# Mixer output projection of a streaming-encoder block: 2x2 blocks by seven products, branch results kept on chip

## Chip, cores and metric

One core of a Trainium2 chip. The metric is the device time of one execution in microseconds (us), from start to end, median of three runs.

## What is computed

One layer in float32 on 512 positions and 1024 channels. `mm` is matrix multiplication over channels; all weights lie in DRAM.

```python
h = rmsnorm(x, norm_mix_g);  z = h @ w_in                  # 1024 -> 7184
a = gmlp_spatial_gating(...); b = forgetting_attention(...)
y_a = a @ w_branch_a;  y_b = b @ w_branch_b                # 1024 -> 1024 each
merged = gate_a * y_a + gate_b * y_b                       # gates: sigmoids of columns of z
x = x + merged @ w_out                                     # the mixer's output projection
h2 = rmsnorm(x, norm_ffn_g);  up = h2 @ w_up               # 1024 -> 5632, then a causal convolution
x = x + (gelu(up[:, :2816]) * up[:, 2816:]) @ w_down
ple = p @ w_ple                                            # 256 -> 1024
x = x + ple * sigmoid(rmsnorm(x, norm_ple_g) @ w_ple_gate)
out = rmsnorm(x, norm_final_g)
```

## The kernel before

Every product is made at close to float32 precision from three passes: an operand is split into a rounded part "hi" and a remainder "lo", and lo*hi, hi*lo and hi*hi are added in a PSUM bank (`mm3`, L166 to L169, and L181/L183/L185, L243/L245/L247 for the two layouts). A matrix 512x1024 times 1024x1024 so takes 192 matmuls with 512 columns each. Splitting a weight piece is a cast on ACT for hi (L153), and for lo either a DVE subtraction (L159) or, with `sub="dma"`, an ACT negation of hi (L156) to which a DMA issued by POOL adds the raw weight (L157, "accumulating DMA"). hi and lo tiles come from a ring of five and one extra, the raw weights from a ring of three.

The order of TensorE's work (PE) is written by hand for most stages, that of ACT, DVE, POOL and of SP's DMA queue is set by a scheduler when the kernel is built; each engine then runs its own list strictly in order, and waits on semaphores for what the others make. Activations live in large SBUF slots numbered 0 to 7; a slot is used anew when its last reader is done.

The stages around the change, with the profile's lines:

- **Branch B** (PE until 432.3 us): eight column tiles of 24 matmuls; `store_b` multiplies the bank by a sigmoid gate (L1039) and POOL writes the result to DRAM as `gyb_d` (L1040). The gates come back from DRAM as `sg` tiles, four buffers (L1019).
- **Branch A** (432.3 to 475.8): the same with `w_branch_a`, whose operand aT is loaded from DRAM in four 1 MB pieces (L992). `store_a` multiplies by the gate (L1052), loads the branch B result (L1054), adds it (L1055) and splits the sum into hi and lo (L380/L381) as mT.
- **Output projection**: `proj_N` for the left 512 columns, 96 matmuls (L167 to L169), all four row blocks at a time; then `proj_N_steps` for the right 512 columns, 96 matmuls row block by row block (L243/L245/L247). `evac_x1` (L1071) adds each bank to x1, the residual. `w_out` comes through the raw ring in eight pieces, each lo made by DVE. In between stand transposes of p (L451) and, row block by row block, `rest[rb]()`: the normed row block is made (L468) and transposed on PE (L421) into h2T.
- **The w_ple product** (24 matmuls) and the **first up-projection**: two gate column tiles ("early"), in halves of 256 columns so that the first half can start before the last row block is there; then the two linear column tiles with 512 columns.
- After that up-projections, convolution and down-projections alternate to the end. The down-projection (L1216) already uses seven products in the place of eight for four groups of its inputs, with the sums for it made by DVE (`pair_parts`).

Of the kernel before, what the change touches and what calls it, by code (L numbers as in the profile page):

```python
# [43 lines left out]
def hybrid_block(  # L44
# [18 lines left out]
    def rows_bc(ap, n):  # L63
# [408 lines left out]
    def k_view(t, n=NK):  # L472
        return t[:, 0:n * 512].rearrange("p (k r) -> p k r", k=n)
# [496 lines left out]


    late_es, late = open_pool("late", "right")
    state["pool"][5] = state["pool"][6] = state["pool"][7] = state["late"] = late
    for i in (5, 6, 7):
        slot(i)
    aT = tuple(k_view(slot(i)) for i in (7, 6))
    cvT = late.tile([P, 2 * P], F32, tag="cvT", name="cvT")
    extra_es, state["extra"] = open_pool("extra", "right")
    for t in ("xhi", "xlo"):
        state["extra"].tile([P, 4, 256], F32R, tag=t, name=uid(t), bufs=1)  # L980
    scr_es, scr = open_pool("scrC", "right")

    oT = tuple(k_view(slot(i)) for i in (2, 3))
# [39 lines left out]
    def branch(wv, act, n0, use, sgs, py=None):  # L1023

        for n in range(0, NK, 2):
            nxt = gates_of(n0 + n + 2) if n0 + n + 2 < N_GATES else None
            py = py or pieces_T(wv, P * n)
# [8 lines left out]
    gyb_d = tc.dram_tile([D, S], F32, name="gyb_d")  # L1036

    def store_b(by, sg, c):
        V.tensor_tensor(sg, by, sg, ALU.mult)  # L1039
        G.dma_start(gyb_d[c * P:c * P + P, :], sg)  # L1040

    sgs = branch(w_b_v, oT, 0, store_b, gates_of(0), w_merge[1])

# [2 lines left out]
        T.transpose(bk[:, i * P:(i + 1) * P], cvr[i], ident)  # L1046
    V.tensor_copy(cvT, bk[:, :2 * P])

    mT = tuple(k_view(slot(i)) for i in (5, 2))
# [12 lines left out]

    scr_es, scr = open_pool("scrD", "right")
    x1 = slot(3, F32).rearrange("p (b c) -> p b c", b=NB)
    nc.sync.dma_start(x1, x2d.rearrange("(b q) c -> q b c", q=P))
    gffn = scr.tile([P, D], F32, tag="gbc", name="gffn", bufs=1)
# [14 lines left out]
    h2T = tuple(k_view(slot(i)) for i in (0, 1))  # L1081


    ple1 = slot(4, F32)[:, 0:2048].rearrange("p (b c) -> p b c", b=NB)
    prep = slot(7)
    pT = tuple(prep[:, 1024 * i:1024 * i + 1024].rearrange("p (k r) -> p k r", k=2) for i in range(2))
    prow = slot(6, F32)[:, 0:1024].rearrange("p (b c) -> p b c", b=NB)
    nc.sync.dma_start(prow, p2d.rearrange("(b q) c -> q b c", q=P))

    def evac_x1b(bk, rb, ch):  # L1090
        evac_x1(bk, rb, ch)
        ss1 = square_sum(bk, x1[:, rb, 512:], "s1")
        rest[rb] = rms_rows(x1[:, rb, :], half[rb], ss1, gffn, scr, h2T, rb)
# [5 lines left out]
    with tc.manual_schedule(engines={mybir.EngineType.PE}):  # L1099
        po = proj_N_steps(w_out_v, 0, NK, mT, 1, evac_x1b)  # L1100
        steps(po, 48)
        transpose_p(prow, pT, 0)
        steps(po, 12)
        rest[0]()
        steps(po, 24)
        rest[1]()
        pp = proj_N_steps(w_ple_v, 0, 2, pT, 1, evac_ple, subs=load_N(w_ple_v, 0, 2, 1))
        steps(po, 12)
        transpose_p(prow, pT, 2)
        w_up0 = [pieces_T(w_up_v, 0, V, "dma")]  # L1110

        up0 = [bank("mm") for _ in range(2)]
        early = chain(*(proj_T_steps(w_up0[0][i], h2T, up0[i], slice(0, 256)) for i in range(2)))
        steps(pp, 16)
        rest[2]()
        steps(pp, 8)
        steps(early, 18)
        rest[3]()
        w_up0.append(pieces_T(w_up_v, DFF, "dma"))
        run(early)  # L1120
        for i in range(2):
            run(proj_T_steps(w_up0[0][i], h2T, up0[i], slice(256, S)))
# [15 lines left out]


    N_SEVEN = 4  # L1140
    A11, A12, A22, S1, S2, S3, S4 = range(7)
    f_last, n_last = 4 * N_SEVEN, NF - 4 * N_SEVEN

    def pair_parts(e, o, t):
# [20 lines left out]
    def up_jobs(q, done):  # L1165

        ug = [None, None]

        def load(o):
            return lambda: pieces_T(w_up_v, o + 2 * q * P, "dma")  # L1170

        def gate(py):
            for i in range(2):
                if q == 0:
                    bk = up0[i]
                else:
                    bk = bank("mm")
                    proj_T(py[i], h2T, bk)
                ug[i] = conv(bk, 2 * q + i, "ug")
                A.activation(ug[i], ug[i], AF.Gelu_apprx_tanh)  # L1180

        def linear(py):
            uls = []
            for i in range(2):
                bk = bank("sc")
                proj_T(py[i], h2T, bk)
# [252 lines left out]
```

## Time and profile before

| | |
|---|---|
| median of 3 runs | 939.83 us (939.01 to 939.87) |
| profiled execution | 939.11 us, of which the span from first to last instruction is 937.3 |
| granted TensorE clock | 0.997 of full speed, mean of the span |
| busy: PE / DVE / ACT / POOL | 923.2 (98%) / 615.9 (66%) / 541.6 (58%) / 98.1 (10%) |
| DMA traffic | 155.84 MB, mean 166 GB/s |

Times in all views are microseconds from the start of the span. A matmul's printed duration is its time from issue to end, and matmuls overlap: the pace is the distance between two starts. "Idle before" in brackets at a row's end is how long the engine stood idle ahead of it, and who released it.

### The profile page before, as it was taken

To read this page: it belongs to the slowest core of one execution; us is meant where nothing else is said; L and a number is where in the kernel's file an instruction comes from. 1 tells how busy PE (TensorE), PEld (TensorE's weight loads), DVE (VectorE), ACT (ScalarE), POOL (GpSimd) and SP (SyncE) were. 2 spreads that over 40 slices of the span, in tenths; PEclk is the share of its full clock that TensorE was granted. 3 is DMA by queue.
4 is the path that set the end of the run, shared out by engine and by line. 5 is a ranking of instruction groups with operands and counts; after the bars stand their busy time and mean duration, and the time that the engine had idled before them with its cause. 6 is when DMAs were issued, how large, how long until landed. Compare 5 with 4: busy or idle time off the path is not lost.

```text
span 937.3 us, 12029 instructions
## 1 busy us (share of the span) xinstructions
PE 923.2 (98%) x4351; PEld 767.3 (82%) x4351; DVE 615.9 (66%) x1121; ACT 541.6 (58%) x868; POOL 98.1 (10%) x152
## 2 busy tenths in 40 slices
PE   8999999999999999999999999999999999999996
PEld 7878888888888888888888888888888888888885
DVE  6886899578777767535635438667666767454654
ACT  7755675477777777434424757656555655545633
POOL 1000001400000001000000211111111111100124
PEclk9999999999999999999999999999999999999998
DMA  9533273756444466399641896684856864975522
GB/s 338 190 91 124 68 205 101 239 154 164 125 116 115 111 158 164 112 352 365 212 156 46 194 258 151 175 192 114 219 139 153 213 149 113 230 233 143 112 69 90
DMA packets 109543, 155.84 MB, mean 166 GB/s; under 512 B 6308, under 2 KB 72028, under 8 KB 109484
## 3 DMA queue, kind: packets, MB, share of 16 engines
q1 hardware_dynamic: 97596, 112.83, 37.6%
q0 software_dynamic: 11744, 41.72, 21.6%
q8 instruction: 34, 0.56, 0.3%
q10 hardware_dynamic: 144, 0.52, 0.1%
q14 instruction: 25, 0.20, 0.1%
HBM read 107.84 MB, written 14.71 MB: 131 GB/s over the span
## 4 chain that ended last, share of the span: by engine, by line
PE 94%; DMA 3%; issue 1%; DVE 1%; ACT 0%; SPq 0%; DVEq 0%; POOLq 0%; POOL 0%
PE bank L181 18%; PE bank L183 18%; PE bank L185 18%; PE bank L1216 8%; PE bank L245 3%; PE bank L243 3%; PE bank L247 3%; PE bank L313 3%; PE bank L320 3%; PE bank L317 3%; PE bank L168 3%; PE bank L169 3%; PE bank L167 3%; PE bank L905 2%; PE bank L896 2%; PE bank L868 1%
## 5 line engine op out<-in xcount | busy, mean ns | idle before, releaser
L181 PE MATMUL bank<-slot,wlo 128*128 128x512 f32 (+1 forms) x664 | 263.4, 398 | 0.0
L183 PE MATMUL bank<-slot,whi 128*128 128x512 f32 (+1 forms) x664 | 258.1, 389 | 0.0
L185 PE MATMUL bank<-slot,whi 128*128 128x512 f32 (+1 forms) x664 | 257.8, 389 | 0.0
L153 ACT CAST whi<-raw 128x1024 fp32r<-128x1024 f32 x100 | 104.6, 1048 | 76.6 <-DMA raw<-in_w_up_dram 19.2
L185 PEld LDWEIGHTS bank<-slot,whi 128*128 128x128 f32 x664 | 124.7, 188 | 25.1
L181 PEld LDWEIGHTS bank<-slot,wlo 128*128 128x128 f32 x664 | 124.7, 188 | 20.6
L183 PEld LDWEIGHTS bank<-slot,whi 128*128 128x128 f32 x664 | 125.1, 188 | 19.6
L157 POOL DMA_DIRECT2D wlo<-raw x54 | 46.8, 866 | 538.8 <-ACT wlo L156 383.9
L159 DVE TENSOR_TENSOR wlo<-raw,whi 128x1024 fp32r<-128x1024 f32 x45 | 55.0, 1223 | 47.3 <-ACT whi L153 47.0
L1216 PE MATMUL bank<-whi,slot 128*128 128x512 f32 x192 | 61.7, 389 | 0.0
L156 ACT ACTIVATE wlo<-whi 128x1024 fp32r<-128x1024 f32 x54 | 57.0, 1059 | 1.0
L245 PE MATMUL bank<-wlo,slot 128*128 128x512 f32 x138 | 54.2, 393 | 0.5 <-DMA wlo<-raw 0.5
L243 PE MATMUL bank<-whi,slot 128*128 128x512 f32 x138 | 54.5, 395 | 0.0
L247 PE MATMUL bank<-whi,slot 128*128 128x512 f32 x138 | 54.1, 392 | 0.0
L1132 DVE SCALAR_TENSOR_TENSOR ul<-bank,cvT,ul 128x511 f32<-128x511 f32 x22 | 16.5, 750 | 41.4 <-ACT ul L1131 41.4
L1216 PEld LDWEIGHTS bank<-whi,slot 128*128 128x128 f32 x192 | 36.0, 188 | 7.4
L878 ACT ACTIVATE t<-t,mn 128x512 f32<-128x512 f32 (+1 forms) x64 | 35.8, 560 | 9.7 <-DVE mn L875 8.3
L265 DVE TENSOR_TENSOR wlo<-slot,whi 128x1024 fp32r<-128x1024 f32 x24 | 29.3, 1221 | 14.9 <-ACT whi L264 14.9
L1131 ACT ACTIVATE ul<-bank,cvT 128x512 f32<-128x512 f32 x22 | 17.1, 775 | 35.6 <-PE bank L185 35.6
L1216 PE MATMUL bank<-wlo,slot 128*128 128x512 f32 x96 | 37.3, 389 | 0.0
L1223 DVE TENSOR_TENSOR slot<-bank,slot 128x512 f32<-128x512 f32 x48 | 32.5, 683 | 5.0 <-PE bank L1216 4.7
L381 DVE TENSOR_TENSOR slot<-bank,slot 128x512 fp32r<-128x512 f32 x34 | 22.5, 684 | 17.8 <-ACT slot L380 17.7
(334 smaller groups left out, 1838.6 us busy)
## 6 DMA issues: line engine op xcount, KB each, us to landing
wlo<-raw POOLq DMA_DIRECT2D x54, 512.0 KB, 5.1
raw<-in_w_up_dram SPq DMA_DIRECT2D x44, 512.0 KB, 4.4
raw<-in_w_in_dram SPq DMA_DIRECT2D x36, 512.0 KB, 3.9
more<-in_w_in_dram SPq DMA_DIRECT2D x20, 512.0 KB, 8.2
slot<-in_w_down_dram SPq DMA_DIRECT2D x16, 512.0 KB, 3.7
raw<-in_w_branch_b_dram SPq DMA_DIRECT2D x8, 512.0 KB, 3.7
slot<-aT_d SPq DMA_DIRECT2D x4, 1024.0 KB, 9.8
sg<-gate_d SPq DMA_DIRECT2D x16, 256.0 KB, 5.2
```

Of the source, the lines that this page charges most:

```text
L153: A.copy(hi, raw)
L156: A.activation(lo, hi.bitcast(F32), AF.Copy, scale=-1.0)
L157: G.dma_start(lo, raw, accum_op=ALU.add)
L159: (sub or V).tensor_tensor(lo, raw, hi.bitcast(F32), ALU.subtract)
L181: T.matmul(out_ap, wl, ah, start=(n == 0 and k == 0), stop=False)
L183: T.matmul(out_ap, wh, al, start=False, stop=False)
L185: T.matmul(out_ap, wh, ah, start=False, stop=end)
L243: T.matmul(bk, alo[:, k, r], wh, start=(k == 0), stop=False)
L245: T.matmul(bk, ahi[:, k, r], wl, start=False, stop=False)
L247: T.matmul(bk, ahi[:, k, r], wh, start=False, stop=(k == nk - 1))
L878: A.activation(t, t, AF.Exp, scale=-1.0, bias=m, accum_out=rs[:, i:i + 1])
L1216: T.matmul(bk, l, m, start=(fresh and k == 0 and n == 0), stop=(k == 1 and n == 2), skip_group_check=not fresh)
```

## The change

- The output projection is computed as a 2x2 block product with seven block products: rows in halves of 256 positions, channels of `merged` in even and odd tiles, columns of `w_out` in halves of 512. Each of the seven is 2 row blocks x 4 channel tiles x 3 passes = 24 matmuls. They accumulate in three pairs of banks (x, y, z); the term that three results share (A11 alone in x) is copied to `m_u` and added to x1 by three accumulating DMAs of 512 KB.
- The sums of activations (parts A11, A12, S1 to S4) are made by DVE and split by ACT and DVE in branch A, after every second column tile (`m_parts`). A22 lies in A12's tile.
- `w_out` is loaded as four 1 MB blocks into slots 0 and 1, once the last gate matmul has read them; sums of blocks are made by DVE (`m_combine`, eight 128x1024 operations). The 14 splits are nine by accumulating DMA and five by DVE; before there were eight by DVE.
- The branch B results stay in SBUF (four "quad" tiles); storing and loading `gyb_d` goes away. In branch A the second weight piece of three of the four pairs is split by accumulating DMA.
- The linear half of the first up-projection is also done in halves of 256 columns; gate tiles have seven buffers; slots are dealt out otherwise (x1 in 6, p and the ple rows in 7).

The core of the diff:

```diff
     def store_b(by, sg, c):
-        V.tensor_tensor(sg, by, sg, ALU.mult)
-        G.dma_start(gyb_d[c * P:c * P + P, :], sg)
+        V.tensor_tensor(gyb(c), by, sg, ALU.mult)
...
+    def m_two(src, i, q, n=2):
+        A.copy(m_at(0, i, q, n), src)
+        V.tensor_tensor(m_at(1, i, q, n), src, m_at(0, i, q, n).bitcast(F32), ALU.subtract)
+
+    def m_parts(e, o, q):
+        e0, e1, o0, o1 = e[:, 0:256], e[:, 256:], o[:, 0:256], o[:, 256:]
+        m_two(e0, A11, q, 1)
+        m_two(o, A12, q)
+        V.tensor_tensor(o1, e1, o1, ALU.add)
+        V.tensor_tensor(e1, e0, e1, ALU.subtract)
+        V.tensor_tensor(e0, o1, e0, ALU.subtract)
+        V.tensor_tensor(o0, o0, e0, ALU.subtract)
+        s23[q] = quad(q)
+        m_two(e, S2, q)
+        m_two(o, S4, q)
...
     def store_a(by, sg, c):
         V.tensor_tensor(sg, by, sg, ALU.mult)
-        gy = scr.tile([P, S], F32, tag="gy", name=uid("gy"), bufs=3)
-        nc.sync.dma_start(gy, gyb_d[c * P:c * P + P, :])
-        V.tensor_tensor(sg, sg, gy, ALU.add)
-        split_out(mT, sg, (slice(None), c, slice(None)))
-
-    branch(w_a_v, aT, NK, store_a, sgs)
+        V.tensor_tensor(sg, sg, gyb(c), ALU.add)
+        if c % 2:
+            m_parts(m_even.pop(), sg, c // 2)
+        else:
+            m_even.append(sg)
...
+    def m_ahead(n):
+        if n == 0:
+            m_load(b11, 0, 0)
+            m_load(b22, 1, 512)
+        elif n == 2:
+            m_load(b12, 0, 512)
+            m_load(b21, 1, 0)
+            m_combine(b12, b22, b12, ALU.subtract)
+        elif n == 4:
+            MERGED.append(m_split(b11, ("dma", "dma"), m_pair))
+            m_combine(b11, b12, b11, ALU.add)
+        elif n == 6:
+            MERGED.append(m_split(b11, ("dma", "dma")))
...
+    branch(w_a_v, aT, NK, store_a, sgs, subs=(None, "dma", "dma", "dma"), after=m_ahead)
...
-    proj_N(w_out_v, 0, NK, mT, 0, evac_x1a, rb_outer=False)
...
+    def m_x(bk, r):
+        evac_x1a(bk, r, 0)
+        if r:
+            for rows, ch in ((2, 0), (2, 1), (0, 1)):
+                G.dma_start(x1[:, rows:rows + 2, 512 * ch:512 * ch + 512], m_u, accum_op=ALU.add)
...
+    w1, w6 = MERGED
+    w2 = m_split(b21)
+    m_product(A11, w1, "x", True, False, m_first)
+    m_product(S2, w6, "y", True, False, qs=range(3))
+    m_combine(b21, b21, b11, ALU.subtract)
+    m_combine(b11, b22, b11, ALU.subtract)
+    m_product(A12, w2, "x", False, True, qs=range(3))
+    m_product(S2, w6, "y", True, False, m_add(2, 0), qs=[3])
+    w5 = m_split(b11, (None, "dma"))
+    m_product(A12, w2, "x", False, True, m_x, qs=[3])
+    A.activation(epst2, half[1], AF.Sqrt)
+    w7 = m_split(b12, ("dma", "dma"))
+    transpose_p(prow, pT, 0)
+    m_product(S1, w5, "y", False, False, m_add(2, 1))
+    w4 = m_split(b21)
+    transpose_p(prow, pT, 2)
+    m_product(S3, w7, "z", True, False, m_x2)
+    w3 = m_split(b22, ("dma", "dma"))
+    m_product(A22, w4, "z", False, True, m_rows(2, 0))
...
+    m_product(S4, w3, "y", False, True, m_rows(0, 1), rs=[0])
+    rest[3]()
+    m_product(S4, w3, "y", False, True, m_rows(0, 1), rs=[1])
```

What stands on the queues as built. **SP's queue at the end of the gates.** In the names, `slot_834`/`slot_835` are the two halves' homes of the w_out blocks, `aT_d` is branch A's operand, `gate_d` the gates. Before:

```order
L150 DMA raw_4080<-in_w_branch_b_dram 128x4x256
L688 DMA gate_d<-gt_3783 128x512
L992 DMA slot_779_3794<-aT_d_650 128x4x512
L992 DMA slot_780_3795<-aT_d_651 128x4x512
L688 DMA gate_d<-gt_3850 128x512
```

With the change:

```order
L150 DMA raw_4083<-in_w_branch_b_dram 128x4x256
L1108 DMA slot_835_4157<-in_w_out_dram 128x4x512
L1108 DMA slot_834_4156<-in_w_out_dram 128x4x512 x2
L1108 DMA slot_835_4157<-in_w_out_dram 128x4x512
L688 DMA gate_d<-gt_3783 128x512
L150 DMA raw_4089<-in_w_branch_b_dram 128x4x256
L150 DMA raw_4164<-in_w_branch_a_dram 128x4x256
L998 DMA slot_778_3793<-aT_d_650 128x4x512
```

Four loads of 1 MB now go ahead of the gates, the last branch B weights, the first branch A weights and aT.

**DVE's queue at the end of branch A.** Column tiles 6 and 7 are `sg_4314` and `sg_4316` before, `sg_4337` and `sg_4339` with the change. Before, L1052/L1055 are the two steps of `store_a`, L381 its split, L159 a split of w_out:

```order
L1052 TENSOR_TENSOR sg_4314<-bank_4407,sg_4314 128x512
L1055 TENSOR_TENSOR sg_4314<-sg_4314,gy_4433 128x512
L381 TENSOR_TENSOR slot_825_4153<-sg_4314,slot_824_4152 128x512
L159 TENSOR_TENSOR wlo_4624<-raw_4622,whi_4623 128x1024
L1052 TENSOR_TENSOR sg_4316<-bank_4439,sg_4316 128x512
L1055 TENSOR_TENSOR sg_4316<-sg_4316,gy_4465 128x512
```

With the change (L1096 and L1097 are `store_a`, L1078 the los of the parts, L1085 to L1088 the sums, L1120 a split and L1126 a sum of w_out blocks):

```order
L1096 TENSOR_TENSOR sg_4337<-bank_4447,sg_4337 128x512
L1087 TENSOR_TENSOR sg_4247<-sg_4249,sg_4247 128x256
L1097 TENSOR_TENSOR sg_4337<-sg_4337,quad_793_3876 128x512
L1088 TENSOR_TENSOR sg_4249<-sg_4249,sg_4247 128x256
L1078 TENSOR_TENSOR quad_868_4418<-sg_4247,quad_868_4418 128x512
L1078 TENSOR_TENSOR slot_833_4155<-sg_4337,slot_833_4155 128x256
L1120 TENSOR_TENSOR wlo_4540<-slot_835_4157,whi_4539 128x1024
L1078 TENSOR_TENSOR slot_831_4153<-sg_4249,slot_831_4153 128x512
L1096 TENSOR_TENSOR sg_4339<-bank_4475,sg_4339 128x512
L1126 TENSOR_TENSOR slot_835_4157<-slot_835_4157,slot_834_4156 128x1024
L1120 TENSOR_TENSOR wlo_4622<-slot_834_4156,whi_4621 128x1024
L1097 TENSOR_TENSOR sg_4339<-sg_4339,quad_793_3876 128x512
```

The sixth of these rows is the last quarter of A11, which the first product reads; between the steps of the two last column tiles stand parts of the pair before and splits and sums of w_out blocks.

**POOL's queue in the output projection**, with the change only (before, it had nothing to issue there). `slot_884` is x1, `slot_885` holds m_u, L1118 is an accumulating split of a w_out block:

```order
L1118 DMA wlo_4516<-slot_834_4156 128x1024
L1118 DMA wlo_4521<-slot_834_4156 128x1024
L1212 DMA slot_884_4529<-slot_885_4530 128x2x512 x2
L1118 DMA wlo_4626<-slot_834_4156 128x1024
L1118 DMA wlo_4647<-slot_834_4156 128x1024
L1212 DMA slot_884_4529<-slot_885_4530 128x2x512
L1118 DMA wlo_4652<-slot_834_4156 128x1024
```

Two of the additions of m_u stand ahead of the second weight piece of S1 (`wlo_4626`), the third ahead of the second piece of S3 (`wlo_4652`).

## Rows read from the trace of the kernel before

**Rows 1.** The page's chain that ended last, share of the span by engine.
```profile
PE 94%; DMA 3%; issue 1%; DVE 1%; ACT 0%; SPq 0%; DVEq 0%; POOLq 0%; POOL 0%
```

**Rows 2.** PE's timeline: start, us, operation; first matmuls of both halves of the projection.
```profile
475.83 0.39 PE L167 MATMUL bank<-whi,slot 128*128 128x512 f32 x1
...
497.59 0.39 PE L243 MATMUL bank<-whi,slot 128*128 128x512 f32 x1
```

**Rows 3.** PE's timeline: the early gate tiles, and the first linear tile.
```profile
534.96 0.28 PE L185 MATMUL bank<-slot,whi 128*128 128x256 f32 x1
536.44 0.38 PE L181 MATMUL bank<-slot,xlo 128*128 128x256 f32 x1 [1.20 <-ACT slot L380]
537.17 0.39 PE L183 MATMUL bank<-slot,xhi 128*128 128x256 f32 x1 [0.34 <-DVE slot L381]
537.39 0.28 PE L185 MATMUL bank<-slot,xhi 128*128 128x256 f32 x1
537.51 0.27 PE L181 MATMUL bank<-slot,xlo 128*128 128x256 f32 x1
...
543.12 0.40 PE L183 MATMUL bank<-slot,whi 128*128 128x512 f32 x1
```

**Rows 4.** The chain of waits ahead of that stall: start, us, what.
```profile
527.36 7.48 DMA raw<-in_w_up_dram
534.86 1.05 ACT whi L153
535.90 0.49 ACT slot L380
```

**Rows 5.** Busy time by window: PE, PEld, DVE, ACT, POOL, then clock, DMA share, GB/s.
```profile
388.70:428.00 39.30, 39.30 (x175) 32.51 (x175) 18.13 (x23) 18.52 (x26) 3.44 (x7) 1.00 0.90 304
432.30:467.00 34.70, 34.70 (x156) 28.71 (x155) 19.86 (x26) 14.95 (x21) 0.54 (x1) 1.00 0.78 267
476.00:498.00 22.00, 22.00 (x98) 18.22 (x98) 8.89 (x11) 7.03 (x12) 0.00 (x0) 1.00 0.49 168
498.00:520.00 22.00, 22.00 (x108) 18.38 (x108) 12.41 (x29) 10.18 (x20) 0.63 (x1) 1.00 0.08 25
```

**Rows 6.** DVE's timeline at the end of branch A.
```profile
470.59 0.69 DVE L1052 TENSOR_TENSOR sg<-bank,sg 128x512 f32<-128x512 f32 x1 [1.99 <-PE bank L185]
...
474.40 1.22 DVE L159 TENSOR_TENSOR wlo<-raw,whi 128x1024 fp32r<-128x1024 f32 x1 [1.01 <-ACT whi L153]
```

**Rows 7.** A group of DVE in 545 to 610: count, busy us and mean ns, idle before.
```profile
L1157 DVE TENSOR_TENSOR sum<-ul 128x256 f32<-128x256 f32 x3 | 1.3, 425 | 0.1
```

**Rows 8.** Groups of ACT in 385 to 545, same columns.
```profile
L153 ACT CAST whi<-raw 128x1024 fp32r<-128x1024 f32 x23 | 24.2, 1051 | 34.9 <-PE bank L169 12.2 <-PE bank L185 11.1 <-DMA raw<-in_w_branch_a_dram 6.7
...
L380 ACT CAST slot<-sg 128x512 fp32r<-128x512 f32 x8 | 4.9, 615 | 10.7 <-DVE sg L1055 10.7
```

**Rows 9.** DMA issues in 388 to 435: KB each, median us to landing.
```profile
slot<-aT_d SPq DMA_DIRECT2D x4, 1024.0 KB, 9.8
...
gyb_d<-sg POOLq DMA_DIRECT2D x8, 256.0 KB, 5.1
```

**Rows 10.** SP's timeline: the first two loads of aT, of four.
```profile
392.61 2.09 SPq L992 DMA_DIRECT2D slot<-aT_d  x2
```

**Rows 11.** Accumulating splits into wlo in 385 to 550.
```profile
DMA to landing us min/median/max: 4.5/6.2/8.2
```

**Rows 12.** The longest accumulating split: DMA issues in 515 to 550.
```profile
xlo<-raw POOLq DMA_DIRECT2D x1, 512.0 KB, 9.3
```

**Rows 13.** POOL's timeline: two accumulating splits.
```profile
519.37 0.89 POOL L157 DMA_DIRECT2D wlo<-raw  x1 [85.58 <-ACT wlo L156]
...
537.64 0.86 POOL L157 DMA_DIRECT2D wlo<-raw  x1 [2.88 <-ACT wlo L156]
```

**Rows 14.** DVE's timeline at the first of them.
```profile
518.92 1.42 DVE L468 SCALAR_TENSOR_TENSOR hn<-slot,ry,gffn 128x512 f32<-128x512 f32 x2
```

More of the change, by code (lines that the diff above doesn't have):

```diff
@@ L972, in hybrid_block @@
     late_es, late = open_pool("late", "right")
-    state["pool"][5] = state["pool"][6] = state["pool"][7] = state["late"] = late
-    for i in (5, 6, 7):
+    state["pool"][6] = state["pool"][7] = state["late"] = late
+    for i in (6, 7):
         slot(i)
@@ L980, in hybrid_block, with quad @@
         state["extra"].tile([P, 4, 256], F32R, tag=t, name=uid(t), bufs=1)
+    quad_es, quads = open_pool("quads", "right")
+    def quad(q, dt=F32R):
+        return quads.tile([P, D], dt, tag=f"q{q}", name=uid(f"quad{q}"))
+    for q in range(4):
+        quad(q)
     scr_es, scr = open_pool("scrC", "right")
@@ L1021, in gates_of, with branch @@
         return sgs
-    def branch(wv, act, n0, use, sgs, py=None):
+    def branch(wv, act, n0, use, sgs, py=None, subs=(None,) * 4, after=None):
         for n in range(0, NK, 2):
             nxt = gates_of(n0 + n + 2) if n0 + n + 2 < N_GATES else None
-            py = py or pieces_T(wv, P * n)
+            py = py or pieces_T(wv, P * n, None, subs[n // 2])
             for i in range(2):
@@ L1033, in branch, with gyb @@
             sgs, py = nxt, None
-        return sgs
-    gyb_d = tc.dram_tile([D, S], F32, name="gyb_d")
+            if after:
+                after(n)
+        return sgs
+    gys = [quad(q, F32) for q in range(4)]
+    def gyb(c):
+        return gys[c // 2][:, 512 * (c % 2):512 * (c % 2) + 512]
     def store_b(by, sg, c):
-        V.tensor_tensor(sg, by, sg, ALU.mult)
-        G.dma_start(gyb_d[c * P:c * P + P, :], sg)
+        V.tensor_tensor(gyb(c), by, sg, ALU.mult)
     sgs = branch(w_b_v, oT, 0, store_b, gates_of(0), w_merge[1])
@@ L1047, in hybrid_block, with m_at @@
     V.tensor_copy(cvT, bk[:, :2 * P])
-    mT = tuple(k_view(slot(i)) for i in (5, 2))
+    A11, A12, A22, S1, S2, S3, S4 = range(7)
+    s41, a_2, a_1 = (slot(i) for i in (2, 3, 4))
+    s23 = [None] * 4
+    M_AT = {A11: (a_1, 256, 0), A12: (a_2, 512, 0), A22: (a_2, 512, 256),
+            S4: (s41, 512, 0), S1: (s41, 512, 256)}
+    def m_at(part, i, q, n=1):
+        if i in (S2, S3):
+            return s23[q][:, 512 * part + 256 * (i == S3):][:, 0:256 * n]
+        t, w, o = M_AT[i]
+        o += 4 * w * part + w * q
+        return t[:, o:o + 256 * n]
@@ new lines, in hybrid_block, with m_load, m_split @@
+    b1, b2 = (slot(i, F32).rearrange("p (h k c) -> p h k c", h=2, k=4) for i in (0, 1))
+    b11, b12, b21, b22 = b1[:, 0], b1[:, 1], b2[:, 0], b2[:, 1]
+    def m_load(b, h, c):
+        nc.sync.dma_start(b, w_out_v[:, h::2, c:c + 512])
+    def m_split(b, subs=(None, None), first=None):
+        res = []
+        for j in range(2):
+            hi, lo = first if first and j == 0 else split_tiles(2, 512)
+            raw = b[:, 2 * j:2 * j + 2]
+            A.copy(hi, raw)
+            if subs[j] == "dma":
+                A.activation(lo, hi.bitcast(F32), AF.Copy, scale=-1.0)
+                G.dma_start(lo, raw, accum_op=ALU.add)
+            else:
+                V.tensor_tensor(lo, raw, hi.bitcast(F32), ALU.subtract)
+            res.append((hi, lo))
+        return res
@@ new lines, in m_combine @@
+    def m_combine(dst, a, b, op):
+        for j in (0, 2):
+            V.tensor_tensor(dst[:, j:j + 2], a[:, j:j + 2], b[:, j:j + 2], op)
+    MERGED = []
+    m_pair = tuple(a_1[:, 2048 + 1024 * t:3072 + 1024 * t].rearrange("p (k c) -> p k c", k=2)
+                   for t in range(2))
+    def m_ahead(n):
[11 more added lines that the diff above has]
+            MERGED.append(m_split(b11, ("dma", "dma")))
@@ L1060, in hybrid_block @@
+    manual = ExitStack()
+    manual.enter_context(tc.manual_schedule(engines={ET.PE}))
+    branch(w_a_v, aT, NK, store_a, sgs, subs=(None, "dma", "dma", "dma"), after=m_ahead)
     scr_es.close()
     scr_es, scr = open_pool("scrD", "right")
-    x1 = slot(3, F32).rearrange("p (b c) -> p b c", b=NB)
+    x1 = slot(6, F32).rearrange("p (b c) -> p b c", b=NB)
+    pT = tuple(a_1[:, 2048 + 1024 * i:3072 + 1024 * i].rearrange("p (k r) -> p k r", k=2)
+               for i in range(2))
+    prep = slot(7, F32)
@@ L1078, in evac_x1a @@
         half[rb] = square_sum(bk, x1[:, rb, 0:512], "s0")
-    proj_N(w_out_v, 0, NK, mT, 0, evac_x1a, rb_outer=False)
[L1081 to L1093, printed above, removed]
     def evac_ple(bk, rb, ch):
@@ L1097, in evac_ple @@
         G.dma_start(ple_d[rb * P:rb * P + P, 512:], ple1[:, rb, :])
[L1099 to L1122, printed above, removed]
+    m_banks = {}
@@ new lines, in m_product @@
+    def m_product(a, ws, acc, fresh, last, evac=None, qs=range(4), rs=range(2)):
+        if acc not in m_banks:
+            m_banks[acc] = [bank({"x": "mm", "y": "sc", "z": "pt"}[acc]) for _ in range(2)]
+        for r in rs:
+            bk = m_banks[acc][r]
+            for q in qs:
+                ah, al = (m_at(t, a, q)[:, P * r:P * r + P] for t in range(2))
+                wh, wl = (w[:, q % 2, :] for w in ws[q // 2])
+                for n, (l, m) in enumerate(((al, wh), (ah, wl), (ah, wh))):
+                    T.matmul(bk, l, m, start=(fresh and q == 0 and n == 0),
+                             stop=(q == 3 and n == 2), skip_group_check=not fresh)
+            if evac:
+                evac(bk, r)
@@ new lines, in m_add, with m_first, m_x2, m_rows @@
+    def m_add(rows, ch):
+        return lambda bk, r: evac_x1(bk, rows + r, ch)
+    def m_first(bk, r):
+        A.copy(m_u[:, r, :], bk)
+    def m_x(bk, r):
[3 more added lines that the diff above has]
+                G.dma_start(x1[:, rows:rows + 2, 512 * ch:512 * ch + 512], m_u, accum_op=ALU.add)
+    def m_x2(bk, r):
+        evac_x1(bk, 2 + r, 1)
+        half[2 + r] = square_sum(m_banks["x"][r], x1[:, 2 + r, 512:], "s1")
+    def m_rows(rows, ch):
+        def f(bk, r):
+            rb = rows + r
+            evac_x1(bk, rb, ch)
+            ss = square_sum(bk, x1[:, rb, 512 * ch:512 * ch + 512], f"s{ch}")
+            rest[rb] = rms_rows(x1[:, rb, :], ss, half[rb], gffn, scr, h2T, rb)
+        return f
@@ new lines, in hybrid_block, with early @@
+    state["turn"], state["bank"] = ["mm", "mm", "av", "pt", "pt", "pt"], 0
+    steps(pp, 16)
+    rest[2]()
+    steps(pp, 8)
+    state["turn"], state["bank"] = ["pt", "av", "pt", "pt"], 0
+    m_product(S4, w3, "y", False, True, m_rows(0, 1), rs=[0])
+    rest[3]()
+    m_product(S4, w3, "y", False, True, m_rows(0, 1), rs=[1])
+    w_up0.append(pieces_T(w_up_v, DFF, V, "dma"))
+    up0 = [[bank(t) for _ in range(2)] for t in ("mm", "sc")]
+    def early(n, i, rows=slice(256, S)):
+        run(proj_T_steps(w_up0[n][i], h2T, up0[n][i], rows))
@@ L1123, in hybrid_block @@
+    early(0, 0)
+    early(0, 1)
+    rest[0]()
+    early(1, 0)
+    rest[1]()
+    early(1, 1)
+    for i in range(2):
+        early(0, i, slice(0, 256))
+    manual.close()
+    state["turn"] = BANK_TURN
     scr_es.close()
+    quad_es.close()
+    five_es, state["pool"][5] = open_pool("five", "right")
+    slot(5)
     scr_es, scr = open_pool("scrE", "right")
@@ L1140, in hybrid_block @@
     N_SEVEN = 4
-    A11, A12, A22, S1, S2, S3, S4 = range(7)
     f_last, n_last = 4 * N_SEVEN, NF - 4 * N_SEVEN
@@ L1184, in linear @@
             for i in range(2):
-                bk = bank("sc")
-                proj_T(py[i], h2T, bk)
+                if q == 0:
+                    bk = up0[1][i]
+                    run(proj_T_steps(py[i], h2T, bk, slice(0, 256)))
+                else:
+                    bk = bank("sc")
+                    proj_T(py[i], h2T, bk)
                 ul = conv(bk, 2 * q + i + NF, "ul")
@@ L1268, in done @@
             if i:
-                tiles[q] = slot((6, 7, 5, 2)[q % 4])
+                tiles[q] = slot((2, 3, 5, 7)[q % 4])
                 pair_parts(*uls, tiles[q])
@@ L1272, in done @@
         if q == 2 * N_SEVEN and i == 0:
-            tiles["last"] = tuple(k_view(slot(n), n_last) for n in (6, 7))
+            tiles["last"] = tuple(k_view(slot(n), n_last) for n in (2, 3))
         split_out(tiles["last"], uls[i], (slice(None), 2 * q + i - f_last, slice(None)))
@@ L1404, in hybrid_block @@
     scr_es.close()
+    five_es.close()
     extra_es.close()
```

19 lines of the change are left out of this document (14 added, 5 removed).

## Prediction

> **What bounds the kernel now.** I read the page's chain first: PE makes up 94% of the chain that ended last [rows 1], so a matmul taken off PE's list is worth its pace, if its place is not taken by a wait. PE's timeline gives the pace: 96 matmuls of 512 columns lie between the starts of the projection's two halves, 475.83 and 497.59 [rows 2], that is 0.2267 us each. The reader is to see there that no bracket stands at the row where the second half begins: PE stood still for nothing. Matmuls of 256 columns follow each other by 0.12 us [rows 3]. The stretch that the change rebuilds reaches from 475.83 to 543.12, where the first linear tile begins [rows 3], and on by its 48 matmuls, to 554.0. In it PE stands still at one place, in two steps: 534.96 + 0.12 = 535.08 to 536.44, and 536.56 to 537.17 [rows 3], together 1.97 us. The chain of waits tells why: a weight load of 7.48 us held an ACT cast to 534.86, and ACT's evacuation of the transposed rows stood behind that cast in its list [rows 4]. By window, DVE is busy 19.86 of 34.7 us in branch A, and 8.89 of 22 in the projection's first half; the clock is 1.00 in each [rows 5].
>
> **PE's part of the change.** The projection has 7 x 24 = 168 matmuls in the place of 192: 24 x 0.2267 = 5.44 us less. The linear tiles' 48 matmuls of 512 columns become 96 of 256: 96 x 0.12 - 48 x 0.2267 = 0.64 us more. Transposes and the w_ple product stay as many, and cancel. The 1.97 us stall: the linear halves that now stand between the last row blocks and the lower halves give ACT and DVE more time. I take the stall as gone, and put in 0.35 us for the one wait that my walk (below) finds in its place. Sum: -5.44 + 0.64 - 1.97 + 0.35 = -6.4 us. The rest of the stretch, some 1 us of small gaps around transposes (67.29 us from 475.83 to 543.12 less 216 x 0.2267, 96 x 0.12, the stall and some 3.9 for transposes), I leave as it is.
>
> **What the other engines get.** Prices: DVE 1.22 us for 128x1024 and 0.69 for 128x512 [rows 6], 0.42 for 128x256 [rows 7]; ACT 1.05 for a 128x1024 cast and 0.62 for 128x512 [rows 8], and I take a negation as a cast.
>
> - DVE, from the end of branch A's first tile (432.3 + 24 x 0.2267 = 437.7) to the use of the last quarter of S2 (475.83 + 60 x 0.2267 = 489.4): 16 steps of `store_a` x 0.69 = 11.0; four pairs, each 5 operations of 128x256 and 3 of 128x512, 4 x 4.17 = 16.7; eight sums of w_out blocks x 1.22 = 9.8; five splits x 1.22 = 6.1. That is 43.6 us of 51.7, or 84%, where it was 57% [rows 5]. It fits, but with little air.
> - ACT, the same stretch: five sigmoids, 16 casts for the parts, about 14 weight casts and 7 negations come to some 36 us, or 70%. It fits too, and is hidden beside PE.
> - DMA: four loads of 1 MB go ahead of the gates and aT on SP. The 4.2 MB take 4.2 / 304 GB/s = 13.8 us at the rate of that window [rows 5]; the eight branch B stores of 256 KB [rows 9] leave it. aT was issued from 392.6 on and took 9.8 us [rows 9, 10], so it moves from about 406 to 420 at worst, and PE wants it at 432.3: hidden, with 12 us left. The gates, later by as much, delay branch B's evacuations, which the eight banks take up.
> - POOL: nine accumulating splits of w_out and three of m_u. Such a DMA lands after 4.5 to 8.2 us, median 6.2 [rows 11]. Adding to x1, which no row shows, I bound by the same rows, 4.5 and 9.3 [rows 12], and take the median: bytes and kind are the same.
>
> **Where it comes close.** I walked the lists of DVE, ACT and POOL as built, each row starting at the later of its predecessor's end and its input. DVE runs without a break from about 460 to 487, and is some 2.5 us behind when tile 6 is done (470.6, [rows 6]). From that:
>
> - last quarter of A11: made at 476.3 to 477.0, used at 475.83 + 9 x 0.2267 = 477.9. Left: about 1.
> - last quarter of S2: made at 486.4, used at 489.4. Left: 3.
> - S1's second weight piece, behind two additions of m_u on POOL: lands at 492 to 493, used at about 494. Left: 1 to 1.5.
> - S3's second piece, behind the third addition, which waits for DVE: lands at about 499.3, used at about 500. Left: 0.7.
> - Row block 2's normed row: ready at 513.4, wanted at 513.1. This is the 0.35 us.
> - First linear tile's lower halves: 534.5 against 535.9. Left: 1.4.
>
> So a late landing of 3 us (9.3 for 6.2) at S1 or S3 shows as 2 to 2.5 us of standstill there; below, no margin turns into a gain, since PE only ever loses what comes late.
>
> POOL's issue row is 0.89 us at 519.37, while DVE runs from 518.92 to 520.34, and 0.86 us later [rows 13, 14]: the row shows no hold by a busy DVE. The Trainium skill ("SBUF — State Buffer", section "SBUF: two separate sides") warns that a DMA issued by GpSimd gets its descriptors from GpSimd, which is locked out of the port pair that it shares with VectorE while VectorE runs a two-port copy, cast or tensor_scalar; `tensor_tensor` has no such mode, by the same page. If a lock held here all the same, each accumulating DMA could be put off by one DVE operation, 1.22 us at most, S3's margin would go, and the sum would be -5.9. By the row it is -6.4, and I stay there.
>
> **Sum.** The profiled execution took 939.11 us: 937.3 of span and 1.8 outside it. With -6.4 it is 932.7; the median lies 0.72 above the profiled run, so the forecast is 939.83 - 6.4 = 933.4.
>
> **Rivals.**
>
> 1. *DVE late at the first products.* With 84% use, a slip of 3 to 5 us passes both A11's and S2's margin, and PE stands still for 2 to 4 us between 477 and 490. For: rows that depend on one another cost a dispatch each, and ACT and DVE wait for one another in every pair. Against: the sum leaves 8 us. It would give 935.4 to 937.4. Chance 0.19.
> 2. *Accumulating DMAs late.* Both S1's and S3's pieces land at the longest time seen: 3.1 - 1.3 + 3.1 - 0.7 = 4.2 us of standstill between 493 and 504, 937.6. For: all go through POOL's one list, and m_u's additions wait for DVE's evacuations. Against: the DMA share there was 0.49 and 0.08 [rows 5], so the landings should be at the short end. Chance 0.09.
> 3. *The gain stops at the next tile.* The second gate tiles' second weight piece was accumulated from 537.64 on [rows 13]; with 6.2 to 9.3 us it lands at 543.8 to 546.9, and was wanted at 554.0. If its loads don't start earlier, it is now wanted at 547.6, with 0.7 to 3.8 us left, and two down-projection weights stand near it on SP. If it comes 2 to 4 us late, the time is 935.4 to 937.4. Chance 0.07.
> 4. *Slower: the w_out loads ahead of everything.* If the 4.2 MB, and the waits of SP behind them, put aT, branch A's weights or the first gates more than 8.3 us beyond 432.3 (6.4 gained and the 1.9 us that a slower kernel needs to be told from no change), the change loses; each us more is a us of time. At 18 us, 432.3 + 18, it is 951; at the edge 941.7. For: DMA share is 0.90 in that window already. Against: by the sum above 12 us are left, so the loads would have to slip by over 20 where 13.8 is their whole price. Chance 0.07.
>
> **The numbers.** Forecast 0.58, with its own range 932.0 to 935.0: below by the small gaps of 1 us that may close, above by one margin that gives. Range 931.9 to 938.0: it takes in rivals 1 to 3, and leaves out rival 4 and what goes wrong twice, some 0.14. A measurement of this kernel can tell 0.2%, 1.9 us, from no change: the forecast and rivals 1 to 3 end below 937.9, but for the tails of the last two, so faster 0.84, same 0.08 (two of the three together), slower 0.08.
>
> **What would show it.** Right: in the profile after, 168 matmuls of the projection's new line, no bracket over 1 us on PE between 475 and 547, and the second gate tiles' first matmul near 547.6 where it was at 554.0. Rival 1 shows as PE waiting for DVE in the new products, with DVE's idle near nothing from 460 on; rival 2 as PE waiting for a DMA into wlo in S1 or S3; rival 3 as a wait for a DMA at 547; rival 4 as PE idle before 475. The forecast is wrong if PE's busy time falls by 5 us and the span does not, or if branch A starts later than 433.

## The result and the profile after

The changed kernel takes 946.29 us (median of 6 runs, 943.61 to 948.11) against 939.85 for the kernel before (6 runs, 938.42 to 940.35): a ratio of 1.007, 95% interval 1.0054 to 1.0087. It is slower by 6.4 us where 6.4 us less was forecast, and lies outside the range given. The profiled execution is its fastest run, 943.61 us, with a span of 941.8 and a mean granted clock of 0.993 (before 0.997). PE's busy time did fall, from 923.2 to 920.9 us; the span rose by 4.5.

The page's chain answers to [rows 1]; "DMA" and "issue" hold what PE lost:

```profile
PE 90%; DMA 5%; issue 3%; DVE 1%; SPq 0%; ACT 0%; POOL 0%; DVEq 0%; POOLq 0%
```

The waits of PE, a view of the whole run: what it waited for, us in total, times, longest. In the stretch from 470 to 560, where before there were the two rows of 1.20 and 0.34 us [rows 3], there are now the first two of these:

```profile
PE bank L421 <- DVE hn L468: 5.1, 1, 5.1
PE bank L1196 <- DMA wlo<-slot: 4.0, 2, 3.4
```

PE's timeline shows where (start, us, operation, idle time ahead of it). L1196 is a matmul of a product, L421 a transpose of a normed row block, L181 to L185 the up-projection:

```profile
475.33 1.52 PE L1196 MATMUL bank<-slot 128*128 128x512 f32 x6
...
493.25 0.63 PE L1196 MATMUL bank<-whi,slot 128*128 128x512 f32 x2
494.44 0.50 PE L1196 MATMUL bank<-wlo,slot 128*128 128x512 f32 x1 [0.56 <-DMA wlo<-slot]
...
500.05 0.63 PE L1196 MATMUL bank<-whi,quad 128*128 128x512 f32 x2
504.07 0.50 PE L1196 MATMUL bank<-wlo,quad 128*128 128x512 f32 x1 [3.40 <-DMA wlo<-slot]
...
535.73 0.28 PE L185 MATMUL bank<-slot,whi 128*128 128x256 f32 x1
541.07 1.94 PE L421 MATMUL bank<-ident,hn 128*128 128x128 f32 x8 [5.05 <-DVE hn L468]
...
545.37 0.41 PE L181 MATMUL bank<-slot,wlo 128*128 128x256 f32 x1
545.58 0.41 PE L183 MATMUL bank<-slot,whi 128*128 128x256 f32 x1
...
558.92 0.40 PE L181 MATMUL bank<-slot,wlo 128*128 128x512 f32 x1
```

Read from start to start, at the paces of before: S1's second weight piece costs 494.44 - (493.25 + 2 x 0.2267) = 0.74 us, S3's second piece 504.07 - 500.50 = 3.57, the normed rows of row block 1 541.07 - 535.85 = 5.22. From 541.07 to the second gate tiles at 558.92 stand 8 transposes (0.79) and 120 matmuls of 256 columns (14.4): 15.2 us of work in 17.85, so 2.6 us went to a lower clock. A table by window says the same: the window and its length, busy time of PE, PEld, DVE, ACT and POOL, then granted clock, DMA share and GB/s:

```profile
490.00:500.00 10.00, 9.44 (x46) 7.48 (x45) 6.37 (x9) 8.94 (x13) 2.40 (x3) 1.00 1.08 195
500.00:504.00 4.00, 0.68 (x3) 0.20 (x2) 0.69 (x1) 1.81 (x3) 1.45 (x2) 1.00 1.05 199
535.00:541.00 6.00, 1.01 (x9) 0.81 (x7) 2.62 (x6) 0.94 (x2) 0.85 (x1) 0.91 1.05 292
541.00:544.00 3.00, 2.94 (x14) 2.97 (x15) 2.81 (x5) 1.17 (x2) 0.00 (x0) 0.50 0.53 158
544.00:547.00 3.00, 3.00 (x17) 3.00 (x16) 0.35 (x1) 0.00 (x0) 0.00 (x0) 0.55 0.48 158
547.00:550.00 3.00, 3.00 (x27) 3.00 (x26) 0.00 (x0) 0.00 (x0) 0.00 (x0) 1.00 0.02 5
```

The sum closes: 932.7 forecast for the profiled run, less 0.35 (the wait expected for row block 2, which did not come) and 0.5 (branch A began that much earlier), plus 0.74 + 3.57 + 5.22 + 2.6, is 944.0; measured were 943.6. All of the loss lies between 490 and 550.

**Why S1's and S3's weights were late.** POOL issued in time; S3's second piece left at 492.97 and landed when PE went on, 504.07, after 11.1 us. POOL's timeline, of the change:

```profile
483.75 2.44 POOL L1212 DMA_DIRECT2D slot<-slot  x2 [15.91 <-ACT whi L1115]
485.22 1.89 POOL L1118 DMA_DIRECT2D wlo<-slot  x1
487.38 0.86 POOL L1118 DMA_DIRECT2D wlo<-slot  x1 [0.27 <-ACT wlo L1117]
492.26 1.20 POOL L1212 DMA_DIRECT2D slot<-slot  x1 [4.03 <-DVE slot L1171]
492.97 1.42 POOL L1118 DMA_DIRECT2D wlo<-slot  x1
```

Six accumulating DMAs of 512 KB and the first of two more follow each other from 483.75 on. From 490 to 504 all 16 DMA engines are busy (share 1.05 to 1.08) at 195 to 199 GB/s, in the windows above; at that rate one takes, by this estimate, 0.524 MB / 197 GB/s = 2.7 us of all the engines. Where plain loads fill them (x1, from 478 to 484) the view by slices shows 338 to 492 GB/s. So, as I read it, each landing waits for those ahead of it. Besides, x1 now lies in slot 6, which held aT: its load could only be issued at 475.30, after branch A, and m_u could not be added before it landed. The experiments below leave that load where it is.

**Why row block 1 was late.** ACT's timeline, one row, and DVE's:

```profile
532.19 1.05 ACT L153 CAST whi<-raw 128x1024 fp32r<-128x1024 f32 x1 [4.84 <-DMA raw<-in_w_up_dram]
```

```profile
533.89 0.16 DVE L463 TENSOR_TENSOR s<-s,s 128x1 f32<-128x1 f32 x1 [5.32 <-ACT bank L457]
...
535.22 0.28 DVE L393 TENSOR_SCALAR rt<-ry,ra 128x1 f32<-128x1 f32 x1
538.78 1.23 DVE L1394 TENSOR_TENSOR slot<-slot 128x1024 f32<-128x1024 f32 x1 [3.28 <-DMA slot<-in_w_down_dram]
539.92 0.21 DVE L394 TENSOR_SCALAR ry<-rt,ry 128x1 f32<-128x1 f32 x1
540.17 1.42 DVE L468 SCALAR_TENSOR_TENSOR hn<-slot,ry,gffn 128x512 f32<-128x512 f32 x2
```

In the midst of the norm's small steps stands L1394, the first sum of w_down blocks for the first down-projection, whose products PE begins only at 591.59, some 50 us later. It waited 3.28 us for its load, and took 1.23. In the kernel before, the same sum stood behind all the norms, where PE did not wait for it:

```profile
554.85 1.23 DVE L1235 TENSOR_TENSOR slot<-slot 128x1024 f32<-128x1024 f32 x1 [6.64 <-DMA slot<-in_w_down_dram]
```

There w_down's block loads went to slot 4 behind the ple rows that lay there, and were issued at 540.91; the change keeps the ple rows in slot 7, so slot 4 comes free sooner, the loads are issued from 520.22 on, and the scheduler moved the sum up into the norm. The sum is not the whole delay: the norm's steps themselves began only at 533.89, since the row's square sum on ACT (L457) stood behind the weight cast that waited for a w_up load to 532.19. An estimate from these rows: without the sum the norm would have gone on at 535.50 in place of 539.92, 4.4 us earlier, and PE would still have waited some 0.8 us. The chain of waits ahead of it (without PE's rows):

```profile
485.22 18.82 DMA wlo<-slot x2
...
515.99 6.75 DMA xlo<-raw
522.76 0.37 SPq L150
523.18 1.16 SPq L1362
524.40 1.04 SPq L1362
525.48 13.21 DMA slot<-in_w_down_dram
538.78 1.23 DVE slot L1394
540.17 0.76 DVE hn L468
```

Two theories follow. Theory 1: two causes that add up, the crowded accumulating DMAs and the sum ahead of the norm. Rival A: the second is an echo of the first, since the chain runs from the one into the other.

### The profile page after: what moved, and what is told of

Its sections match the earlier page's. It is cut to its first block, busy times and chain, and to the rows that moved or that the text cites. A ratio compares the mean times of both kernels' runs of the same rounds, so it can differ in the third digit from the quotient of the medians.

```text
span 941.8 us, 12133 instructions
## 1 busy us (share of the span) xinstructions
PE 920.9 (98%) x4375; PEld 767.3 (81%) x4375; DVE 630.2 (67%) x1152; ACT 562.2 (60%) x896; POOL 107.0 (11%) x158
## 4 chain that ended last, share of the span: by engine, by line
PE 90%; DMA 5%; issue 3%; DVE 1%; SPq 0%; ACT 0%; POOL 0%; DVEq 0%; POOLq 0%
PE bank L181 17%; PE bank L183 17%; PE bank L185 17%; PE bank L1375 8%; PE bank L313 3%; PE bank L317 3%; PE bank L320 3%; PE bank L245 3%; PE bank L247 3%; PE bank L243 3%; DMA wlo<-slot 2%; PE bank L905 2%; PE bank L896 2%; PE bank L168 2%; PE bank L169 2%
## 5 line engine op out<-in xcount | busy, mean ns | idle before, releaser
L181 PE MATMUL bank<-slot,wlo 128*128 128x512 f32 (+1 forms) x696 | 273.4, 394 | 0.0
L183 PE MATMUL bank<-slot,whi 128*128 128x512 f32 (+1 forms) x696 | 268.0, 385 | 0.0
L185 PE MATMUL bank<-slot,whi 128*128 128x512 f32 (+1 forms) x696 | 267.7, 385 | 0.0
L185 PEld LDWEIGHTS bank<-slot,whi 128*128 128x128 f32 x696 | 131.7, 189 | 25.2
L181 PEld LDWEIGHTS bank<-slot,wlo 128*128 128x128 f32 x696 | 131.9, 190 | 20.5
L183 PEld LDWEIGHTS bank<-slot,whi 128*128 128x128 f32 x696 | 132.2, 190 | 19.6
L153 ACT CAST whi<-raw 128x1024 fp32r<-128x1024 f32 x95 | 99.4, 1048 | 44.7 <-PE bank L185 15.9
L159 DVE TENSOR_TENSOR wlo<-raw,whi 128x1024 fp32r<-128x1024 f32 x38 | 47.2, 1245 | 28.2 <-ACT whi L153 27.9
L1375 PE MATMUL bank<-whi,slot 128*128 128x512 f32 x176 | 56.5, 389 | 0.0
L245 PE MATMUL bank<-wlo,slot 128*128 128x512 f32 x106 | 41.7, 394 | 0.1
L243 PE MATMUL bank<-whi,slot 128*128 128x512 f32 x106 | 41.7, 394 | 0.0
L247 PE MATMUL bank<-whi,slot 128*128 128x512 f32 x106 | 41.5, 392 | 0.0
L1375 PEld LDWEIGHTS bank<-whi,slot 128*128 128x128 f32 x176 | 33.0, 188 | 6.8
L264 ACT CAST whi<-slot 128x1024 fp32r<-128x1024 f32 x22 | 23.0, 1045 | 18.9 <-PE bank L185 15.3
L1375 PE MATMUL bank<-wlo,slot 128*128 128x512 f32 x88 | 34.2, 389 | 0.0
```

What stands on the lines that cost most here:

```text
L153: A.copy(hi, raw)
L159: (sub or V).tensor_tensor(lo, raw, hi.bitcast(F32), ALU.subtract)
L181: T.matmul(out_ap, wl, ah, start=(n == 0 and k == 0), stop=False)
L183: T.matmul(out_ap, wh, al, start=False, stop=False)
L185: T.matmul(out_ap, wh, ah, start=False, stop=end)
L243: T.matmul(bk, alo[:, k, r], wh, start=(k == 0), stop=False)
```

## Experiments

All compare with the kernel before on the same chip; 943.6 and 946.3 are the changed kernel's profiled run and median. The first four ran on one chip and the last four on another; the kernel before took 939.57 and 938.77 us there, so medians across the two compare to about 1 us.

**m_u added by DVE.** Six additions in the place of the three accumulating DMAs:

```diff
+    def m_plus(rb, ch, r):
+        t = x1[:, rb, 512 * ch:512 * ch + 512]
+        V.tensor_tensor(t, t, m_u[:, r, :], ALU.add)
+
     def m_add(rows, ch):
-        return lambda bk, r: evac_x1(bk, rows + r, ch)
+        def f(bk, r):
+            evac_x1(bk, rows + r, ch)
+            m_plus(rows + r, ch, r)
+            if ch:
+                m_plus(r, 1, r)
+        return f
...
-        if r:
-            for rows, ch in ((2, 0), (2, 1), (0, 1)):
-                G.dma_start(x1[:, rows:rows + 2, 512 * ch:512 * ch + 512], m_u, accum_op=ALU.add)
```

> The three accumulating DMAs that add m_u to x1 become six DVE additions of 128x512; nothing else changes. Theory 1 (two separate waits: the seven accumulating DMAs between 484 and 504 fill the DMA engines, so that S1's and S3's weight pieces come late; the DVE sum of w_down blocks that stands ahead of the normed rows is a cause of its own): PE's waits for a DMA in L1196 (4.0 us) fall below 0.5, the wait for hn stays at about 5, the profiled run comes to about 939.3. Rival A (the second wait is only the echo of the first): both go, 931 to 933. Rival B (the accumulating DMAs are slow for another reason, as x1's late load): the waits in L1196 stay above 3 us.

Measured: median 939.95 (ratio to before 1.0005, 0.9994 to 1.0016), 6.3 us below the changed kernel; the profiled run 940.38. In its waits between 470 and 565 only one row is left:

```profile
PE bank L421 <- DVE hn L468: 5.3, 1, 5.3
```

The waits in L1196 are gone, against rival B, and the wait for hn stays, against rival A: it moved ahead with PE and did not shrink. Here the norm's steps were in time (L463 at 528.04), and the sum alone, which waited for its load to 535.58, held them.

**The w_down loads later.** A tiny DVE copy into their target, which reads the transposed rows, so that the loads and with them the sum come after these:

```diff
         def ready0():
+            if g == 0:
+                V.tensor_copy(raws[:, :, 0, 0:1], h2T[1][:, 0:4, P:P + 1].bitcast(F32))
             load()
```

> The first four w_down loads wait until the first row blocks' h2T is written, by a tiny DVE copy into their target; the sum of w_down blocks on DVE so falls behind all normed rows. Theory 1: the wait for hn (5.1 us) goes and with it the drop of the granted clock behind it; the waits in L1196 stay at 4.0; profiled run 943.6 - 5.2 - 2.6 = 935.8. Rival C (the clock drop is not tied to that wait): only 5.2 us go, 938.4.

Measured: median 938.18 (0.9988, 0.9976 to 1.0), 8.1 below the changed kernel; the profiled run 936.37. The only wait left between 470 and 565, and then, by window, the stretch where the clock had been 0.50:

```profile
PE bank L1196 <- DMA wlo<-slot: 3.9, 2, 3.4
```

```profile
541.00:544.00 3.00, 3.00 (x28) 3.00 (x27) 0.00 (x0) 0.64 (x1) 0.00 (x0) 1.00 0.45 132
```

The clock stays at 1.00 when the wait for hn is gone, so the 2.6 us belong to that wait: 5.2 + 2.6 = 7.8 were expected and 7.2 (profiled) to 8.1 (medians) measured, against rival C.

**Both edits.**

> Both edits together. Theory 1: no wait over 1 us on PE between 475 and 550, first matmul of the second gate tiles near 547, profiled run about 931.5 to 932.5, median 933 or below, faster than both kernels. If a further wait stands behind these two (the second gate tiles' weights, the rows' norm), 934 to 938.

Measured: median 931.96 (6 runs, 931.35 to 933.05), ratio 0.9923, 0.9908 to 0.9937, faster than both kernels. PE waits for nothing between 470 and 565, and the second gate tiles begin at

```profile
547.87 0.40 PE L181 MATMUL bank<-slot,wlo 128*128 128x512 f32 x1
```

where the forecast had 547.6. Measured each alone, the two gains, 6.3 and 8.1, add up to 14.4; both together gave 946.3 - 932.0 = 14.3. That is theory 1.

**Only the order on DVE.** A one-column operation that reads b12 and the transposed rows stands ahead of the sum; loads and SP's list stay:

```diff
             w1 = split_w(b11)
+            if g == 0:
+                V.tensor_tensor(scr.tile([P, 1], F32, tag="dd", name="dd", bufs=1), b12[:, 0, 0:1],
+                                h2T[1][:, 0, P:P + 1].bitcast(F32), ALU.add)
             V.tensor_tensor(b12, b22, b12, ALU.subtract)
```

> Only the order on DVE changes: the sum of w_down blocks is held behind the normed rows by a one-column DVE operation ahead of it; w_down's loads and SP's list stay as they are. Theory 1: as with the loads put off, the wait for hn goes and the clock stays: profiled run about 935.8. Rival D (the loads' traffic in 520 to 540 is what makes the rows late, not the order on DVE): the wait for hn or another DMA wait of 2 to 5 us remains, 938 to 943.

Measured: median 939.82 (1.0008, 0.9991 to 1.0025), 6.5 us below the changed kernel, where putting off the loads gave 8.1; the profiled run 940.15. Both lie in rival D's range. The wait for hn is 2.5 us instead of 5.1, with a clock of 0.62 from 541 to 544. What is left stands on ACT: a cast of an up-projection weight waits for its load, with the row's square sum (L457) behind it:

```profile
533.97 1.05 ACT L153 CAST whi<-raw 128x1024 fp32r<-128x1024 f32 x1 [6.70 <-DMA raw<-in_w_up_dram]
534.92 0.59 ACT L457 ACTIVATE bank<-slot 128x512 f32<-128x512 f32 x1
```

So rival D has its part: DVE's order is most of the loss, a late w_up load the rest. How the 5.1 us divide is not fixed by this: the load held that cast to 533.97, 1.8 us longer than in the changed kernel (532.19).

**The same order with m_u on DVE**, to tell whether that load was late for w_down's traffic or as an echo of the accumulating DMAs:

> m_u added by DVE, and the sum of w_down blocks held behind the normed rows, with w_down's loads where they are. The order alone left 2.5 us of waiting for hn when the other stall was there. If that rest is the loads' traffic in 520 to 540 (a w_up load of 11.2 us holding an ACT cast, with the row's square sum behind it): it stays, and since PE comes 4 us earlier it is 2.5 to 6 us, the time 935 to 940. If it was an echo of the late accumulating DMAs: no wait, 932.

Measured: median 933.2 (0.9944, 0.9927 to 0.9962). The wait for hn is 1.4 us, the clock 1.00; that ACT cast now waits to 528.47, 5.5 us earlier, where PE is about 4.4 us earlier. Neither expectation fits exactly: of the 2.5 us, 1.1 went with the late accumulating DMAs, and 1.4 stayed. With w_down's loads put off as well (both edits) no wait is left, so their traffic is the likely cause of these 1.4; it is not shown, since with m_u on DVE alone, amid the same loads, that cast went on at 526.34.

**Copies in the place of additions.** The three DMAs of m_u lose `accum_op`, which leaves x1 without the residual in three quarters:

> The three DMAs of m_u into x1 only copy, they do not add (x1 then lacks the residual in three quarters: that part of the computation is changed); queue, order, bytes and issue stay. Between 490 and 500 the accumulating DMAs filled the 16 engines at 195 GB/s, where plain loads between 478 and 488 ran at about 420. Theory 1 (an accumulating DMA costs the engines about twice a plain one): three copies take some 3 x 1.3 us less, S3's second piece lands about 4 us earlier, and PE's waits in L1196 fall from 4.0 to under 1. Rival E (they are slow because two weight pieces, x1's load and POOL's order coincide, whatever the kind): the waits stay at 3 to 4 us.

One run: 939.93 us, and the waits in L1196 are gone. From 483 to 500, first in the changed kernel, then in this one: what POOL's DMA queue moved (packets, MB, share of the 16 engines' time), and its issues (KB each, median us to landing):

```profile
q0 software_dynamic: 1138, 2.77, 92.7%
wlo<-slot POOLq DMA_DIRECT2D x4, 512.0 KB, 9.6
slot<-slot POOLq DMA_DIRECT2D x3, 512.0 KB, 7.3
```

```profile
q0 software_dynamic: 864, 3.15, 74.2%
wlo<-slot POOLq DMA_DIRECT2D x4, 512.0 KB, 6.2
slot<-slot POOLq DMA_DIRECT2D x3, 512.0 KB, 4.7
```

Same queue, order and bytes of each: more bytes moved in less of the engines' time, so that they add is what filled the engines. Rival E falls. An estimate from the two queue lines, over 17 us: 15.8 us of the engines for 2.77 MB is 3.0 us for a DMA of 0.524 MB that adds; 12.6 us for 3.15 MB, half of it the three copies, leaves 1.2 us for a copy. (The expectation's 420 GB/s for plain loads holds from 478 to 482 only; from 483.75 on the accumulating DMAs run.)

**The changed kernel again.**

> The changed kernel once more beside the others. Median near 946; waits of 4.0 us in L1196 and 5.1 us for hn, granted clock under 0.7 for some 6 us behind the second, as in its first profile.

Measured: 947.3 (1.0088, 1.0068 to 1.0107), waits of 4.4 and 5.3 us. Its window from 500 to 510 had a clock of 0.83, where the first profile had 1.00: the wait at S3 can cost clock too, which would fit the 2.7 us by which the median lies above the first profile; that was seen in one profile and not tried further.

**Linear tiles whole**, on the kernel with both edits:

```diff
-    up0 = [[bank(t) for _ in range(2)] for t in ("mm", "sc")]
+    up0 = [[bank("mm") for _ in range(2)]]
...
-    early(1, 0)
     rest[1]()
-    early(1, 1)
...
-                if q == 0:
-                    bk = up0[1][i]
-                    run(proj_T_steps(py[i], h2T, bk, slice(0, 256)))
-                else:
-                    bk = bank("sc")
-                    proj_T(py[i], h2T, bk)
+                bk = bank("sc")
+                proj_T(py[i], h2T, bk)
```

> On the kernel with both edits, the first two linear tiles are done whole again, with 512 columns, after the gate tiles; the last two row blocks' transposes then come directly behind the gate's upper halves. Theory 1 (the linear halves are what hides the last two row blocks): the 0.64 us of short matmuls comes back, but PE waits for hn or for the transposed rows by 2 to 6 us, and the time is 2 to 6 us above the kernel with both edits (932.0): 934 to 938, more if the clock falls. Rival F (the row blocks are ready in time anyway): 931.4.

Measured: 935.77 (0.9967, 0.9958 to 0.9977), 3.8 above the kernel with both edits. The waits come back, 1.9 us for hn and 0.5 for the transposed rows: the short linear halves pay for their 0.64 us. 2.4 - 0.64 = 1.8 us is what the profiled runs differ by (934.26 and 932.60, 1.7 us); the other 2 us of the medians were not traced. The mean clock of the runs behind this median, 0.994 to 0.996 where the kernel with both edits has 0.997, points at the clock.

## Why the prediction was wrong

- *PE's part: right in size.* 24 matmuls less, 0.64 us for the short halves, the old stall gone: with both waits taken away the stretch ends at 547.87 against 547.6, and the profiled run takes 932.60 against 932.7 (median 931.96 against 933.4). The single terms were not measured apart.
- *The step that failed first: "Adding to x1 ... I bound by the same rows ... and take the median", and with it S3's margin of 0.7.* The landings of 4.5 to 8.2 us [rows 11] came from a stretch in which such DMAs start 2.9 us apart or more. Eight of them in 20 us fill the engines, at 2.7 us each, and the splits' landings came to 9.6 in the median and 11.1 at S3. Rival 2 named this place and priced it at 4.2 us, against 4.3 measured. That the sums agree is luck: the rival's parts were 1.8 for S1 and 2.4 for S3, measured were 0.74 and 3.57, and S3's piece took 11.1 us to land, above the 9.3 that the rival took for the longest. It got a chance of 0.09, because I argued from the DMA shares of 0.49 and 0.08 [rows 5]. Those are shares of the kernel before, where none of the change's accumulating DMAs run.
- *The step that failed worst: "I take the stall as gone".* I looked at what the linear halves hide, and at the rows on PE, but not at what else the scheduler had put into DVE's list there. The sum of w_down blocks stands inside the norm's steps in the list as built. The prediction names neither it nor the wait for its load, which landed after 13.2 us; the margins of its walk, down to the 1.4 us of the last line, leave that wait out. In its place PE stood still for 5.2 us. The kind of stall was the old one (a row block behind weight work that waits for a load), now mainly on DVE and in part still on ACT. Nothing in the rivals had it, nor the 2.6 us of clock behind it. The range left out "what goes wrong twice"; two things went wrong.
- *Rival 1* (DVE late at the first products): did not come. DVE's use from 437.7 to 489.4 was 36.7 of the 51.7 us, or 71%, where the sum had 84%. A11, S2 and A12 run without a bracket; DVE made A11's last quarter by 475.2 (its row: 474.82 and 0.42 us), a little before my 476.3.
- *Rival 3* (second gate tiles' weights): did not come; with both edits PE reaches them at 547.87 and does not wait.
- *Rival 4* (w_out's loads ahead of everything): did not come. Branch A began at 431.70, 0.5 us earlier than before. The slower side was real, but by a mechanism that I had not listed.
- *The rule on GpSimd's descriptors*, from the Trainium skill ("SBUF — State Buffer", section "SBUF: two separate sides"): no run shows a hold that decides. In the changed kernel some issue rows that follow each other closely are longer than 0.86 us (1.20, 1.42, 1.89), but with m_u on DVE all of them are 0.86 from 487 to 503, beside a DVE that is busy 8.92 of the 10 us from 490 to 500, all of it with `tensor_tensor`; the rule's two-port operations were not tried. The delay was in the DMA engines, behind the issue.

## What to carry to other kernels

A DMA's time from issue to landing is not its price: when a change puts several in a row, add up what each takes of the engines (here about 2.7 us for 512 KB that are added, and by the estimate above under half of that for a copy), and use the traffic of the kernel after, not before. When a change gives slots new tenants, look for what comes free earlier, and follow each load that then starts sooner to the operation that waits for it: here DVE, which runs its list in order, let that wait fall on the norm behind it. The margin of 0.7 us behind a DMA was gone with one landing of 11.1 us in the place of 6.2.

## What was not expected of the hardware

- An accumulating DMA within SBUF ran at about half the rate of a load: 195 to 199 GB/s at full engines against 338 to 492 in the slices of 478 to 484.
- The clock after a wait: none was lost behind waits of 1.4 and 1.9 us, nor, in the first profile, behind 3.4 us between matmuls of 512 columns; it fell in the window behind 3.5 us in another profile of the same kernel, and behind 2.5 us (0.62 in 541 to 544, with only the order on DVE changed) and 5.1 us (0.50 in 541 to 544) at the norm. At 0.50, the lower of its two levels, the 256-column matmuls follow each other by 0.21 us in place of 0.12.
